# First feed-forward product as 2x2 block products with seven multiplications, and modulation products moved to layer 2

## The chip, the core and the metric

One core of a Trainium2 chip runs the whole program. The metric is device time in microseconds (us) of one execution; the kernel before takes 2892.97 us in the median of three runs, from 2887.84 to 2894.72. The engines are TensorE (PE in the rows; PEld is its weight load), VectorE (DVE), ScalarE (ACT), GpSimd (POOL), and SyncE (SP), which issues all loads and stores. Each engine takes its instructions in the order in which they stand in its queue.

## What is computed

Two layers of a diffusion backbone work on 128 context and 512 latent tokens together, 640 columns. Each layer mixes tokens in three branches (latent attention, gated linear attention, gated DeltaNet) and then applies a SwiGLU feed-forward. Both parts are shifted, scaled and gated by a modulation vector that comes from a condition through its own weights:

```python
mod = silu(cond) @ w_mod[l] + b_mod[l]
sh_a, sc_a, g_a, sh_f, sc_f, g_f = split(mod, 6)
h = h + g_a * mixer(rmsnorm(h, norm_mix) * (1 + sc_a) + sh_a)
xf = rmsnorm(h, norm_ffn) * (1 + sc_f) + sh_f
gu = xf @ ffn_w_in[l]                    # 1024 -> 2 x 2816
h = h + g_f * ((silu(gu[..., :2816]) * gu[..., 2816:]) @ ffn_w_out[l])
```

## The kernel before

Activations stand with 128 channels on the partitions and the 640 tokens along the free axis, in two halves of 320. Every large product is made in three matmuls, to keep float32's precision in a faster format: the weight piece is split by `wsplit` into a rounded part `wh` (ScalarE, L465) and a residue `wl` (GpSimd, L466), the activation likewise into `xh` and `xl`, and `mm_k` (L474) adds wh times xh, wh times xl, wl times xh. A weight piece holds four blocks of 128x128 and so covers 512 of the contracted channels; a tile of a 1024-channel product takes two pieces, 8 blocks x 3 products x 2 halves = 48 matmuls of 320 columns.

The order of these products is fixed: `job` lists them, and class `Stream` (object `G`) emits them piece by piece between other work. Three weight buffers of each kind rotate, so a piece can be split while the two before it are in use; loads run two pieces ahead. `G.to(name)` emits products until the named one is done, `fill` emits as many as a table gives for a place, and when a tile is done its post (a function in `G.posts`) is emitted. A scheduler then sets each engine's order by priorities; steps of the modulation carry a call that keeps them in program order.

The feed-forward has 22 column pairs in two groups of eleven. For pair f, tile `fg` (gate) and tile `fu` (up) are multiplied, `g_post` (L1765, L1766) makes SiLU from a tanh, `u_post` (L1773) multiplies, and `split` (L478 VectorE, L479 GpSimd) makes the operand pair `ah`, `al` of the second product `fo`, which follows each group with eight tiles. `h_update` (L637) adds each into the residual. The feed-forward's input comes from `modulate`, by halves of the tokens, once the norm of the last residual tile is there (`join`); L619 and L622 scale, L624 (ScalarE) and L631 (VectorE) make `xh` and `xl`.

The modulation has 48 columns of 128 for each of two conditions. The first 16 of layer 1 are made by TensorE at the start. All others are dot products on VectorE: one instruction (L549) multiplies a row of weights `wmt` by the condition and sums it, and a short second one reads the sum. Layer 1 makes its 20 next columns between the steps of its DeltaNet chain (rows halved to 512), four more during the output projection `wo`, and in its feed-forward the last eight and all 48 of layer 2 (rows of 1024). Layer 2 makes none itself.

## Time and profile before

| | us |
|---|---|
| median of three runs | 2892.97 |
| span of the profiled execution | 2896.0 |
| chain stage of layer 1, 623.42 to 896.30 | 272.88 |
| chain stage of layer 2, 2058.95 to 2324.19 | 265.24 |
| feed-forward start to the first gate tile's post, layer 2, 2407.60 to 2427.25 | 19.65 |
| pairs 12 to 22 of the first product, layer 1, 1222 to 1377 | 155.00 |
| pairs 12 to 22 of the first product, layer 2, 2650 to 2805 | 155.00 |

For the profiled execution the span is the time that is known, from its first to its last instruction; it lies 3.0 us above the median of the runs. The chain stage runs here from the clearing of a buffer (L1710) to the first operand of the last merge (L1528).

### The profile page before, as it was taken

Reading aid. Unit: us, or ns where it says so; the run is one execution under the profiler, and the core shown is the slowest. Engines: PE = TensorE matmul, PEld = TensorE weight load, DVE = VectorE, ACT = ScalarE, POOL = GpSimd, SP = SyncE. Lnnn points to the kernel's source line nnn. Section 1 sums busy time; section 2 is a strip of 40 time slices with the busy share of each in tenths; the row PEclk is TensorE's granted clock in tenths of the full one; section 3 lists DMA queues with packets and bytes.
Section 4 is the critical chain, followed back from the end, with each engine's and each line's share of the span. In section 5 each row is a group of like instructions: output and inputs, shape, how many; then the busy total and the mean of one; then the engine's idle time right before and its main releaser. Section 6 shows DMA issues by size and latency. Waiting matters only on the chain. (4 is left out here: it accounts for less than half of the span.)

```text
span 2896.0 us, 49763 instructions
## 1 busy us (share of the span) xinstructions
PE 2721.4 (94%) x19444; PEld 2498.5 (86%) x19444; DVE 1542.6 (53%) x2834; ACT 1209.0 (42%) x2276; POOL 1196.0 (41%) x872
## 2 busy tenths in 40 slices
PE   7899999889999999999998899987999999999998
PEld 4788888778779899999988888876877898999998
DVE  4765584747655699177358576556334334211212
ACT  5575655543333522122366645554333344222223
POOL 3543222333325467366445323233333264443443
PEclk9999999999999999999999999998999999999999
DMA  6254433245433355344323534332423231222222
GB/s 207 90 161 141 91 82 94 88 130 168 140 101 127 108 189 177 86 139 156 105 84 110 177 90 97 72 93 73 137 79 88 73 111 59 77 73 78 73 74 83
DMA packets 291834, 317.10 MB, mean 109 GB/s; under 512 B 163696, under 2 KB 174768, under 8 KB 291472
## 3 DMA queue, kind: packets, MB, share of 16 engines
q1 hardware_dynamic: 291600, 313.92, 37.3%
q8 instruction: 154, 2.52, 0.4%
q14 instruction: 80, 0.66, 0.1%
HBM read 266.01 MB, written 47.82 MB: 108 GB/s over the span
## 5 line engine op out<-in xcount | busy, mean ns | idle before, releaser
L466 POOL TENSOR_TENSOR wl<-wr,wh 128x512 fp32r<-128x512 f32 (+1 forms) x576 | 813.9, 1416 | 1307.0 <-ACT wh L465 1177.0
L474 PE MATMUL gm<-xh,wh 128*128 128x320 f32 x3456 | 846.2, 322 | 25.1 <-ACT xh L624 9.4
L474 PE MATMUL gm<-xh,wl 128*128 128x320 f32 x3456 | 826.8, 316 | 13.4 <-POOL wl L466 13.4
L474 PE MATMUL gm<-xl,wh 128*128 128x320 f32 x3456 | 832.5, 317 | 7.2 <-DVE xl L631 4.2
L465 ACT ACTIVATE wh<-wr 128x512 fp32r<-128x512 f32 (+1 forms) x576 | 357.6, 623 | 944.0 <-PE gm L474 648.9
L474 PEld LDWEIGHTS gm<-xh,wh 128*128 128x128 f32 x3456 | 589.6, 192 | 52.5 <-ACT xh L624 14.5
L474 PEld LDWEIGHTS gm<-xl,wh 128*128 128x128 f32 x3456 | 594.3, 192 | 25.0 <-DVE xl L631 9.8
L474 PEld LDWEIGHTS gm<-xh,wl 128*128 128x128 f32 x3456 | 592.6, 192 | 21.7 <-POOL wl L466 15.5
L549 DVE CUSTOM_DVE_ANT_0 ctb<-wmt,cbb 128x1024 f32<-128x1024 f32 (+1 forms) x200 | 298.6, 1493 | 3.4
L637 DVE SCALAR_TENSOR_TENSOR h<-gm,mod,h 128x128 f32<-128x128 f32 x144 | 55.7, 462 | 272.2 <-PE gm L474 266.1
L474 PE MATMUL gm<-ah,wh 128*128 128x320 f32 x704 | 164.6, 310 | 0.5 <-DVE h L637 0.5
L474 PE MATMUL gm<-ah,wl 128*128 128x320 f32 x704 | 164.1, 309 | 0.0
L474 PE MATMUL gm<-al,wh 128*128 128x320 f32 x704 | 163.9, 309 | 0.0
L962 ACT ACTIVATE VN<-ch 64x64 f32<-64x64 f32 x320 | 70.0, 219 | 178.5 <-DVE vs L959 164.5
L474 PEld LDWEIGHTS gm<-ah,wh 128*128 128x128 f32 x704 | 118.7, 188 | 1.6 <-DVE h L637 1.5
L474 PEld LDWEIGHTS gm<-al,wh 128*128 128x128 f32 x704 | 118.5, 188 | 0.2
L474 PEld LDWEIGHTS gm<-ah,wl 128*128 128x128 f32 x704 | 118.5, 188 | 0.0
L1773 DVE TENSOR_TENSOR th<-th,gm 128x640 f32<-128x640 f32 x44 | 36.2, 822 | 149.2 <-PE gm L474 148.4
L1766 DVE SCALAR_TENSOR_TENSOR th<-th,gm 128x640 f32<-128x640 f32 x44 | 35.9, 816 | 138.3 <-ACT th L1765 138.3
L479 POOL TENSOR_TENSOR al<-th,ah 128x640 fp32r<-128x640 f32 x44 | 89.5, 2033 | 28.0 <-DVE ah L478 28.0
L474 PE MATMUL gm<-ol,wh 128*128 128x320 f32 x384 | 99.3, 332 | 1.5 <-POOL ol L479 1.5
L474 PE MATMUL gm<-oh,wh 128*128 128x320 f32 x384 | 98.7, 334 | 0.5 <-DVE gth L1524 0.3
(747 smaller groups left out, 3822.8 us busy)
## 6 DMA issues: line engine op xcount, KB each, us to landing
wr<-in_wall_dram SPq DMA_DIRECT2D x432, 256.0 KB, 3.0
wmt<-in_wmodt_dram SPq DMA_DIRECT2D x60, 512.0 KB, 3.7
wr<-in_wfo_dram SPq DMA_DIRECT2D x64, 256.0 KB, 2.6
wr<-in_wbr_dram SPq DMA_DIRECT2D x48, 256.0 KB, 2.7
wmt<-in_wmodt_dram SPq DMA_DIRECT2D x40, 256.0 KB, 3.2
wm<-in_wmod_dram SPq DMA_DIRECT2D x16, 512.0 KB, 8.3
wr<-in_wfo_dram SPq DMA_DIRECT2D x32, 192.0 KB, 2.4
h<-in_xt_dram SPq DMA_DIRECT2D x16, 320.0 KB, 5.5
```

The costliest lines, as they stand in the source:

```text
L465: se.activation(wh[:, :w], wr[:, :w], AF.Copy)
L466: ge.tensor_tensor(wl[:, :w], wr[:, :w], wh[:, :w], op=ALU.subtract)
L474: pe.matmul(ps[:, c, :HF], w_[:, wsl], x_[kx][:, c * HF:(c + 1) * HF], start=(start and i == 0), stop=(stop and i == 2))
L479: (lo or ge).tensor_tensor(dst_l, src, dst_h, op=ALU.subtract)
L549: ins = ve.tensor_tensor_reduce(self.t, wm, self.c[:, i], 0.5, 0.0, ALU.mult, ALU.add, accum_out=acc[h][:, m - m0, i:i + 1])
L637: ve.scalar_tensor_tensor(hs[d][:, s:e], ps[:, c, s - c * HF:e - c * HF], g[:, d, i:i + 1], hs[d][:, s:e], op0=ALU.mult, op1=ALU.add)
L962: se.activation(VN[d * 64:(d + 1) * 64, h, n], ps[h * 64:(h + 1) * 64, 1], AF.Copy)
L1766: ve.scalar_tensor_tensor(v3(th), v3(th), 1.0, ps, op0=ALU.add, op1=ALU.mult)
L1773: ve.tensor_tensor(v3(th), v3(th), ps, op=ALU.mult)
```

## The change

The first product's weights of one pair, gate above and up below, form a 2x2 block matrix of 128x512 blocks: A11 and A12 for the gate, A21 and A22 for the up part, by the two halves of the contracted channels. The input forms one too: B11 and B21 for the first half of the tokens, B12 and B22 for the second. For 20 of the 22 pairs the four output blocks are now made from seven block products instead of eight, after Winograd: sums of weight blocks S1 to S4 and of input blocks T1 to T4 are multiplied, and the products are combined. A block product is 4 blocks x 3 products x 1 half = 12 matmuls. The first two pairs stay as they were. The 22 pairs now stand in three groups of eight, seven and seven.

The sums S1 to S4 are made per pair on VectorE (L519), the sums T once per layer after the modulation (`token_sums`). Of the seven weight pieces of a pair two have their residue made by GpSimd and five by VectorE (L494). ScalarE copies three partial results out of PSUM (L1933), VectorE combines them (L1939, L1945, L1948) and then makes SiLU and the product (L1951 to L1953). `ah` is now made by ScalarE (L1911) and `al` by VectorE (L1912). Layer 2 now makes its own modulation columns 16 to 47 at the places where layer 1 makes its own, and layer 1's feed-forward makes only its first 16; all rows are halved to 512 there, with three row buffers instead of four.

```diff
-GROUPS = ((0, 11), (11, 22))
+GROUPS = ((0, 8), (8, 15), (15, 22))
+NPL = 2
...
+PRODS = {1: ("A11", "B11", 0, True), 2: ("A12", "B21", 1, True), 6: ("S2", "T2", 0, False), 5: ("S1", "T1", 1, True),
+         7: ("S3", "T3", 0, False), 4: ("A22", "T4", 0, False), 3: ("S4", "B22", 1, False)}
...
+    def product(self, pair, prod, pre=None):
+        wn, xs, bank, start = PRODS[prod]
+        i = self._sub((pair.name, prod), lambda: pair.get(wn), 4, "pool" if prod in (1, 2) else "dve")
+        self.units.append(dict(name=pair.name, i=i, k0=0, kn=4, xs=xs, c=bank, last=prod == 3, pre=pre, prod=prod, start=start))
...
-    def wsplit(wr, kt):
+    def wsplit(wr, kt, lo=None):
...
-            ge.tensor_tensor(wl[:, :w], wr[:, :w], wh[:, :w], op=ALU.subtract)
+            (ve if lo == "dve" else ge).tensor_tensor(wl[:, :w], wr[:, :w], wh[:, :w], op=ALU.subtract)
...
+    class Pair:
+        def __init__(self, name, top, low):
+            self.name, self.t = name, {}
+            self.src = {"A11": top[:, 0:512], "A12": top[:, 512:1024], "A21": low[:, 0:512], "A22": low[:, 512:1024]}
+        def get(self, n):
+            if n not in self.t:
+                if n in self.src:
+                    if n in ("A11", "A12"):
+                        self.t[n] = wload(self.src[n])
+                    else:
+                        with prio("pl"):
+                            self.t[n] = cur["sw"].tile([P, 512], F32, name="wq", tag="wq", bufs=3)
+                            dma(self.t[n], self.src[n])
+                else:
+                    x, y, op = {"S1": ("A21", "A22", ALU.add), "S2": ("S1", "A11", ALU.subtract),
+                                "S3": ("A11", "A21", ALU.subtract), "S4": ("A12", "S2", ALU.subtract)}[n]
+                    x, y = self.get(x), self.get(y)
+                    with prio("pw"):
+                        self.t[n] = cur["sw"].tile([P, 512], F32, name="ws", tag="ws", bufs=5)
+                        ve.tensor_tensor(self.t[n], x, y, op=op)
+            return self.t[n]
+        def fetch(self, *names):
+            for n in names:
+                self.get(n)
+    def mm_block(ps, w, k, xs, start, stop):
+        wsl = slice(k * P, (k + 1) * P)
+        h, l_ = cur["X"][xs]
+        with prio("pg"):
+            for i, (w_, x_) in enumerate(((w[0], h), (w[0], l_), (w[1], h))):
+                pe.matmul(ps, w_[:, wsl], x_[k], start=(start and i == 0), stop=(stop and i == 2),
+                          skip_group_check=True)
...
+    def token_sums(us, sh, xeh, xel, xt1, pool_):
+        h0, h1 = HS
+        for k in range(4):
+            for d in (k, k + 4):
+                for i, s, e in ((0, 0, TP), (1, TP, T)):
+                    se.activation(us[d][:, s:e], us[d][:, s:e], AF.Identity, bias=sh[:, d, i:i + 1])
+            u, v, t1 = us[k], us[k + 4], xt1[:, k]
+            t = pool_.tile([P, 3, HF], F32, name="tsum", tag="tsum", bufs=2)
+            ve.tensor_tensor(t1, u[:, h1], u[:, h0], op=ALU.subtract)
+            ve.tensor_tensor(t[:, 0], v[:, h1], t1, op=ALU.subtract)
+            ve.tensor_tensor(t[:, 1], v[:, h1], u[:, h1], op=ALU.subtract)
+            ve.tensor_tensor(t[:, 2], v[:, h0], t[:, 0], op=ALU.subtract)
+            se.activation(xeh[:, k], t, AF.Copy)
+            ve.tensor_tensor(xel[:, k], t, xeh[:, k], op=ALU.subtract)
...
+            q = pairs[fs[0]]
+            G.product(q, 1, lambda q=q: q.fetch("S1", "S2"))
+            G.product(q, 2, lambda q=q: q.fetch("S3", "S4"))
+            kf = f1 - f0
+            for f in fs:
+                q, n = pairs[f], pairs[f + 1] if f + 1 < f1 else None
+                G.product(q, 6)
+                G.product(q, 5)
+                G.product(q, 7, n and (lambda n=n: n.fetch("A21", "A22")))
+                if n:
+                    G.product(n, 1)
+                else:
+                    fo(0, [(0, 4)])
+                G.product(q, 4, n and (lambda n=n: n.fetch("S1", "S2")))
+                if n:
+                    G.product(n, 2, lambda n=n: n.fetch("S3", "S4"))
+                G.product(q, 3)
+            fo(1, [(0, 4)])
+            fo(0, [(4, kf - 4)])
+            fo(1, [(4, kf - 4)])
+            for d in range(2, 8):
+                n = pairs[f1] if d == 7 and gi + 1 < len(GROUPS) else None
+                fo(d, pre=n and (lambda n=n: n.fetch("A21", "A22")))
...
-                    mst = ModVe(bd, 4, 2).steps(0, range(16, 16 + OPT["mc"])) if l == 0 else iter(())
+                    mst = ModVe(bd, 4, 2).steps(l, range(16, 16 + OPT["mc"]))
...
-        mv = ModVe(mvp, 4, 1) if l + 1 < L else None
+        mv = ModVe(mvp, 3, 2)
...
+        mvs = mv.steps(l, range(16 + OPT["mc"], 40), True)
...
+            own = mv.steps(l, range(40, 48), True)
+            nxt = mv.steps(l + 1, range(16), True) if l + 1 < L else iter(())
...
+            def close(f, f0, f1, th):
+                se.activation(ah[:, f - f0], th, AF.Copy)
+                ve.tensor_tensor(al[:, f - f0], th, ah[:, f - f0], op=ALU.subtract)
+                if f0 == 0:
+                    some(own, 4 if f + 1 < f1 else 1000)
+                    if f + 1 == f1:
+                        mod_fix(mod, prm, 5)
+                elif f1 < NF:
+                    some(nxt, 2)
...
+                def post(prod, ps):
+                    def kept(n):
+                        s_[n] = sn.tile([P, HF], F32, name="sn", tag="sn", bufs=3)
+                        se.activation(s_[n], ps[:, 0, :HF], AF.Copy)
+                    if prod == 1:
+                        kept(1)
+                    elif prod == 2:
+                        g.append(tmp())
+                        ve.tensor_tensor(g[0][:, h0], ps[:, 1, :HF], s_[1], op=ALU.add)
+                    elif prod == 6:
+                        kept(2)
+                    elif prod == 7:
+                        kept(3)
+                        u = sn.tile([P, HF], F32, name="su", tag="su", bufs=1)
+                        ve.tensor_tensor(u, ps[:, 1, :HF], s_[3], op=ALU.add)
+                        g.append(u)
+                    elif prod == 3:
+                        ve.tensor_tensor(g[0][:, h1], ps[:, 1, :HF], s_[2], op=ALU.add)
+                        th = tmp()
+                        se.activation(th, g[0], AF.Tanh, scale=0.5)
+                        ve.scalar_tensor_tensor(th, th, 1.0, g[0], op0=ALU.add, op1=ALU.mult)
+                        ve.tensor_tensor(th[:, h0], th[:, h0], ps[:, 0, :HF], op=ALU.mult)
+                        ve.tensor_tensor(th[:, h1], th[:, h1], g[1], op=ALU.mult)
+                        close(f, f0, f1, th)
+                return post
+            gl_ = len(GROUPS) - 1
...
+            def fo_post(gi, d):
+                def post(ps):
+                    h_update(hs, d, ps, mod[:, 40:48])
+                    some(nxt, 3 if (gi, d) != (gl_ - 1, 7) else 1000)
                 return post
...
+            se.activation(xh[:, 0:4, HF:], xt1, AF.Copy)
+            ve.tensor_tensor(xl[:, 0:4, HF:], xt1, xh[:, 0:4, HF:], op=ALU.subtract)
```

How the change moves instructions, at two places. On ScalarE at the start of layer 1's feed-forward, before: the last pieces of the input (xh, L624) with the weight pieces (wh, L465) between and behind them, then the tanh of the first gate tile.

```order
L624 ACTIVATE xh<-th,mod_102 128x320 x6
L465 ACTIVATE wh<-wr 128x512
L624 ACTIVATE xh<-th,mod_102 128x320 x2
L465 ACTIVATE wh<-wr 128x512
L1765 ACTIVATE th<-gm 128x640
L465 ACTIVATE wh<-wr 128x512 x4
```

The same place now; us are the scaled input tiles, xeh the rounded token sums, wh (L493) the weight pieces of the first two pairs.

```order
L705 ACTIVATE xh<-us_10060,mod_102 128x320
L705 ACTIVATE xh<-us_10061,mod_102 128x320
L715 ACTIVATE us_10058<-us_10058,mod_102 128x512
L715 ACTIVATE us_10059<-us_10059,mod_102 128x128
...
L722 ACTIVATE xeh<-tsum 128x960
L715 ACTIVATE us_10061<-us_10061,mod_102 128x128
L722 ACTIVATE xeh<-tsum 128x960
L715 ACTIVATE us_10061<-us_10061,mod_102 128x512
L493 ACTIVATE wh<-wr 128x512 x2
L1905 ACTIVATE th<-gm 128x640
```

The weight piece that stood ahead of the last two input pieces now stands behind 14 instructions of the token sums, of L715 and L722.

On VectorE in the first group of layer 1, before: a pair's two posts and the cast, then modulation steps of 1024 columns.

```order
L1766 SCALAR_TENSOR_TENSOR th<-th,gm 128x640
L1773 TENSOR_TENSOR th<-th,gm 128x640
L478 CAST ah<-th 128x640
L549 ISA ctb,mod_103<-wmt,cbb 128x1024
L549 ISA mod_103 128x1
L549 ISA ctb,mod_103<-wmt,cbb 128x1024
L549 ISA mod_103 128x1
L549 ISA ctb,mod_103<-wmt,cbb 128x1024
```

Now, in the third pair of the first group: al, wl, su and th are operands of the pairs, L614 the modulation steps of 512 columns; the weight sums (L519) and more residues (L494) stand above and below.

```order
L1951 SCALAR_TENSOR_TENSOR th<-th 128x640
L1952 TENSOR_TENSOR th<-th,gm 128x320
L1953 TENSOR_TENSOR th<-th,su 128x320
L1912 TENSOR_TENSOR al<-th,ah 128x640
L614 ISA ctb,mod_102<-wmt,cbb 128x512
L614 ISA mod_102 128x1
L494 TENSOR_TENSOR wl<-wq,wh 128x512
L614 ISA ctb,mod_102<-wmt,cbb 128x512
L614 ISA mod_102 128x1
L614 ISA ctb,mod_102<-wmt,cbb 128x512
L614 ISA mod_102 128x1
L1945 TENSOR_TENSOR su<-gm,sn 128x320
```

The steps stand after the pair's last residue (L1912), and the residues of the next products (L494) and the partial sum (L1945) now stand between them in the same queue.

## Rows read from the trace of the kernel before

**Rows 1.** The page's first part, the span and the engines' totals
```profile
span 2896.0 us, 49763 instructions
...
PE 2721.4 (94%) x19444; PEld 2498.5 (86%) x19444; DVE 1542.6 (53%) x2834; ACT 1209.0 (42%) x2276; POOL 1196.0 (41%) x872
```

**Rows 2.** Stretches: us, busy us (count) of PE, PEld, DVE, ACT, POOL, clock, DMA
```profile
1222.00:1377.00 155.00, 155.00 (x1059) 155.00 (x1058) 113.87 (x122) 34.37 (x56) 95.12 (x55) 1.00 0.46 144
...
2650.00:2805.00 155.00, 155.00 (x1059) 155.00 (x1058) 31.05 (x35) 34.46 (x56) 72.78 (x54) 1.00 0.26 76
```

**Rows 3.** TensorE's instructions in order: start, us, engine, line, operation; output projection, layer 2
```profile
2394.09 0.31 PE L474 MATMUL gm<-xh,wh 128*128 128x320 f32 x1
...
2397.47 0.31 PE L474 MATMUL gm<-xh,wl 128*128 128x320 f32 x1
```

**Rows 4.** VectorE in order, end of output projection and start of feed-forward, layer 2
```profile
2389.20 0.83 DVE L598 TENSOR_TENSOR nacc<-nacc,th 128x640 f32<-128x640 f32 x1 [0.81 <-ACT th L597]
...
2407.26 0.48 DVE L619 TENSOR_TENSOR th<-us,nacc 128x320 f32<-128x320 f32 x1
...
2427.97 0.82 DVE L1766 SCALAR_TENSOR_TENSOR th<-th,gm 128x640 f32<-128x640 f32 x1 [1.89 <-ACT th L1765]
```

**Rows 5.** VectorE in order, feed-forward of layer 1
```profile
1306.23 0.82 DVE L1773 TENSOR_TENSOR th<-th,gm 128x640 f32<-128x640 f32 x1 [3.09 <-PE gm L474]
...
1308.26 1.21 DVE L549 CUSTOM_DVE_ANT_0 ctb<-wmt,cbb 128x1024 f32<-128x1024 f32 x1
1309.40 0.08 DVE L549 DVE_READ_ACCUMULATOR2_ANT mod<- 128x1 f32 x1
1309.51 2.48 DVE L549 CUSTOM_DVE_ANT_0 ctb<-wmt,cbb 128x1024 f32<-128x1024 f32 x1
...
1312.04 2.20 DVE L549 CUSTOM_DVE_ANT_0 ctb<-wmt,cbb 128x1024 f32<-128x1024 f32 x1
```

**Rows 6.** GpSimd in order, the same stretch
```profile
1306.69 1.30 POOL L466 TENSOR_TENSOR wl<-wr,wh 128x512 fp32r<-128x512 f32 x1 [2.22 <-ACT wh L465]
...
1313.74 1.66 POOL L466 TENSOR_TENSOR wl<-wr,wh 128x512 fp32r<-128x512 f32 x1 [0.58 <-ACT wh L465]
```

**Rows 7.** ScalarE in order, start of the feed-forward, layer 2
```profile
2394.68 0.40 ACT L613 ACTIVATE us<-h,mod 128x128 f32<-128x128 f32 x1
2395.46 0.74 ACT L597 ACTIVATE th<-h 128x640 f32<-128x640 f32 x1 [0.38 <-DVE h L637]
2396.11 0.71 ACT L613 ACTIVATE us<-h,mod 128x512 f32<-128x512 f32 x1
...
2423.28 0.63 ACT L465 ACTIVATE wh<-wr 128x512 fp32r<-128x512 f32 x1 [1.14 <-PE gm L474]
2423.82 1.00 ACT L624 ACTIVATE xh<-th,mod 128x320 fp32r<-128x320 f32 x2
```

**Rows 8.** VectorE in order, the first pair's second half done, layer 2
```profile
2431.70 0.82 DVE L1773 TENSOR_TENSOR th<-th,gm 128x640 f32<-128x640 f32 x1 [2.91 <-PE gm L474]
```

**Rows 9.** Lines by form: shapes xcount | busy us, mean ns | idle before
```profile
L1111 ACT ACTIVATE kbh<-pkn 64x768 fp32r<-64x768 f32 x16 | 12.8, 801 | 5.2 <-DVE kbl L1112 5.0
...
L549 DVE CUSTOM_DVE_ANT_0 ctb<-wmt,cbb 128x512 f32<-128x512 f32 x80 | 69.1, 864 | 0.3
```

**Rows 10.** Stretches, as rows 2: chain stages, output projections and norms, start of feed-forward
```profile
623.42:896.30 272.88, 265.99 (x2219) 218.65 (x2218) 164.96 (x487) 90.85 (x245) 96.74 (x79) 0.99 0.49 136
2058.95:2324.19 265.24, 259.29 (x2210) 214.87 (x2209) 101.14 (x318) 88.38 (x242) 91.32 (x78) 0.99 0.36 97
896.30:998.17 101.87, 95.50 (x592) 90.66 (x590) 64.58 (x98) 51.05 (x91) 56.84 (x38) 0.93 0.43 142
2324.19:2427.25 103.06, 97.27 (x602) 92.23 (x600) 46.47 (x79) 49.83 (x88) 53.39 (x38) 0.93 0.28 89
2407.60:2427.25 19.65, 16.58 (x68) 13.91 (x68) 15.67 (x33) 12.96 (x27) 6.33 (x6) 0.71 0.04 10
```

**Rows 11.** DMA issues: line, engine, operation xcount, KB each, us to landing
```profile
wr<-in_wall_dram SPq DMA_DIRECT2D x432, 256.0 KB, 3.0
```

184 lines of the change are left out of this document (115 added, 69 removed).

## Prediction, made before the changed kernel was run

> **What bounds the kernel now.** I read the page's totals first: TensorE is busy for 94% of the span and no other engine for more than 53% [rows 1]. An average hides stages with other limits, so the view by stretches came next, cut at the edges of the feed-forward in the timeline. The reader should see that the stretch from 1222 to 1377 us, eleven of the 22 column pairs of layer 1's first feed-forward product, has TensorE busy in all of its 155.00 us, and that layer 2's, 2650 to 2805 us, is as long to the digit although VectorE is busy for 113.87 us in one and 31.05 in the other [rows 2]. So TensorE alone sets this stage, and everything else lies beside it. 155.00 us over 1059 matmuls is 0.146 us each; 1056 of them are the eleven pairs, so a pair of 96 costs 14.1 us. The new products use single halves of 320 columns; TensorE already does that at the end of the output projection, where the first and the last of 24 such matmuls start 3.38 us apart, 0.147 each [rows 3]. The price holds for the new form.
>
> **What is removed.** Twenty of the 22 pairs of each layer fall from 96 to 84 matmuls: 12 x 20 x 2 = 480 x 0.1464 = 70.3 us of TensorE time. A pair is then 84 x 0.1464 = 12.3 us of TensorE, if the weights arrive in time. The second product, the first two pairs and the number of their weight pieces do not change.
>
> **What VectorE gets for it.** Per pair the order shows nine instructions of 128x512 (four weight sums at L519, five residues at L494), five of 128x320 (L1939, L1945, L1948, L1952, L1953) and two of 128x640 (L1951, L1912). Prices when GpSimd is out of the way: 0.48 us for 320, 0.83 for 640, hence 0.69 for 512 on the line between [rows 4]. That is 9 x 0.69 + 5 x 0.48 + 2 x 0.82 = 10.3 us. A next instruction that does not wait starts 0.07 before the end of the one before (1308.26 + 1.21 against 1309.40, [rows 5]); over some 14 joins that is 1.0 off, 9.3 us. To this come two waits. The residue at L1912 follows a ScalarE copy of 640 columns that itself follows VectorE's last product, and the queue is in order: the like of it costs 0.81 us of idle time at 2389.20 [rows 4]. And GpSimd: where one of its residues meets VectorE's steps, a step of 1.21 becomes 2.20, 0.99 more, and the residue 1.66 instead of 1.30 [rows 5, 6]. A pair keeps two on GpSimd, and about 0.8 of VectorE's work in it reads SBUF alone (four of the 0.48 read PSUM, and L1773, which does so now, keeps its 0.82 while a residue of GpSimd runs into it and keeps its 1.30 [rows 5, 6]); 2 x 0.99 x 0.8 = 1.6. Together 9.3 + 0.8 + 1.6 = 11.7 us against 12.3 of TensorE: hidden, with 0.6 to spare. The bounds are 10.1 (the two never meet) and 12.6 (both always do, at 2.48 - 1.21 = 1.27 each). ScalarE's seven splits and five other instructions of at most 640 columns are under 7 x 0.63 + 5 x 0.74 = 8.1 us a pair [rows 7] and stay beside it.
>
> **The modulation steps on top of it.** A step of 512 columns is 0.69 plus 0.04 for reading its sum (1309.51 - 1308.26 against 1.21, [rows 5]), 0.73.
> - First group, both layers: the order puts 24 steps and two refreshes of the condition (0.69 each) in the six pairs' rows, 18.9 us or 3.2 a pair. 11.7 + 3.2 = 14.9 against 12.3: VectorE becomes the bound, and as a product's weights are made at most two products ahead (three buffers), nothing averages this out. 2.6 x 6 = 15.6 a layer, 31 us in both. Bounds: 6 a layer from 10.1, 21 from 12.6.
> - Second group, layer 1: 15 steps in seven pairs, 1.6 each; 13.3 against 12.3, 7 us. Bounds 0 and 13.
> - The other groups carry no steps: 0, or up to 0.3 x 21 = 6 us from 12.6. Steps between the second product's tiles hide: such a tile is 48 matmuls, 7.0 us of TensorE, for three steps and one update.
>
> **The start of the feed-forward.** Before, ScalarE makes the weight piece of the first pair's second half at 2423.28, ahead of the last two pieces of the input, and the pair's post comes at 2431.70; TensorE did its last 24 matmuls, 3.5 us, just before, so it began them near 2428.1 [rows 7, 8]. In the new order that piece stands behind the token sums: 14 rows of L715 and L722 lie between the last input piece and it, six of 0.71, five of 0.40 and three of 960 columns (1.0 each, drawn on from 0.80 for 768) [rows 7, 9], 9.3 us. Here too a next one starts 0.09 early (2395.46 + 0.74 against 2396.11), 13 times, and 8.1 us are left; five more lie before the last input piece, in time that ScalarE spends waiting for GpSimd now. The sums that VectorE must finish first (12 of 320 columns and one residue of 960, 6.4 us) keep just ahead of it. Input done near 2425.2, plus 8.1, the piece's own 0.63 and about 0.5 of mutual waits: 2434.4 against 2428.1, 6.3 us without work for TensorE in each layer, 13 us. Bounds: 0 (the sums fit into gaps), and 10 a layer, since after the wait for the norm the clock stands at a mean of 0.71 in these 20 us [rows 10] and a second stop could keep it low.
>
> **The modulation in layer 2.** Its chain stage gets 80 steps of 0.864 us [rows 9]. Layer 1 has had them there all along: from the same clearing of a buffer to the same first merge it takes 272.88 us, layer 2 without them 265.24 [rows 10]. I take the 7.6 difference as their price. Layer 1's output projection, with steps, takes 101.87 against 103.06, so there they hide [rows 10]. Bounds 0 and 15, for the points where this layer's products are filled in were set without them.
>
> **Sum.** -70.3 + 31 + 7 + 13 + 7.6 = -12 us. It is made against the profiled execution (2896.0 us of span); the runs before stand at 2893 in the median, and I move the difference there: **2881 us**.
>
> **Rivals.**
> - VectorE keeps pace. For it: GpSimd does half as much per pair as before, so the two may seldom meet; at 10.1 us a pair, the first group still loses 12 us and the second nothing. -70.3 + 12 + 13 + 7.6 = -38, 2855; with the start hidden as well 2842. Against it: in layer 1 now VectorE's steps of 1024 columns are 1.21, 2.48 and 2.20 one after the other [rows 5], so they do meet when VectorE is full.
> - The meeting costs the whole of GpSimd's instruction each time: pair 12.6, first group 3.5 x 6 x 2 = 42, second 13, the others 6, then -70.3 + 42 + 13 + 6 + 13 + 7.6 = +11, 2904, slower. It decides as soon as a pair without steps exceeds 12.3. For it: one step of 2.48 [rows 5]. Against it: the next costs 0.99. [...]
> - The weights come late. All loads stand in SyncE's one queue; a modulation row waits there until VectorE has used the row three loads before it, and the weight loads behind it wait too. With VectorE 2.6 us late per pair, one landing of 3.0 us [rows 11] would be laid open in each of the first group's six pairs: 2 x 6 x 3.0 = 36, 2881 + 36 = 2917, slower. For it: the order has a modulation row ahead of weight rows throughout that group. Against it: two pieces are always loaded ahead, and with weights landing in 3.0 us TensorE shows no wait for one now.
>
> **Numbers.** Forecast 0.46, VectorE keeping pace 0.24, whole exclusion 0.17, late weights 0.13. The forecast's own range is 2866 to 2896. This kernel's runs spread so that less than 0.3%, about 8.7 us, can't be told from no change; 2884.3 and 2901.7 are the edges. Faster: 0.24 and 0.6 of 0.46, 0.52. Same: 0.35 of 0.46 and 0.2 of 0.17, 0.19. Slower: the rest, 0.29. The range runs from the first rival to the last: 2844 to 2914.
>
> **What the new profile would show.** The matmul count down by 480 and TensorE at 0.146 to 0.147 where it is fed. If I am right: in the first group of both layers a pair near 14.9 us with VectorE busy over 90%, TensorE waiting there for residues of L494; the last group of layer 2 near 12.3 a pair without waits; a stop of 6 us for a weight piece of L493 soon after each feed-forward's start; layer 2's chain stage near 273 us. I am wrong if the first group's pairs run at 12.3 or 13, if pairs without steps lie over 12.6, or if TensorE's waits name a weight's DMA.

## The result and the profile after

The changed kernel takes 2969.45 us in the median (2961.4 to 2970.32) against 2893.84 (2887.84 to 2897.18) for the kernel before, measured beside it: a ratio of 1.025, interval 1.0229 to 1.0271. The forecast was 2881, with a range to 2914. The profiled execution took 2961.4 us, the lowest of the four; its span is 63.3 us longer than before, while the medians lie 75.6 us apart, and the stages below can account for the 63.3 alone.

The totals, as in [rows 1]:

```profile
span 2959.3 us, 50253 instructions
...
PE 2691.0 (91%) x18964; PEld 2439.6 (82%) x18964; DVE 1888.7 (64%) x3712; ACT 1390.0 (47%) x2624; POOL 988.0 (33%) x748
```

The 480 matmuls are gone (19444 to 18964), and TensorE is busy for 30 us less. It is idle for 94 us more, and no other engine comes near its span. So the work became less and the waits more; the stages say where. Their edges are read from TensorE's timeline, where one product's matmuls end and the next one's begin (us; "tiles" are the first product's column tiles of each group, the two products that the order puts between them included; "mixer 2" runs from the end of layer 1's feed-forward to layer 2's output projection; the other names are those of the experiments):

```
                 projection    norm         tiles, layer 1       tiles, layer 2       mixer 2
before           54.1  53.0    9.9   9.9    164.7  154.9         164.7  154.9          895.6
changed          59.1  59.0   17.0  16.5    142.1  104.4   99.8  141.9  100.2  100.1   901.4
1 order held     59.1  59.0   17.1  17.2    144.7  103.8   99.9  144.8  100.3  100.3   905.2
2 table held     58.6  59.3    9.9   9.9    149.0  106.0   99.8  145.1   99.9   99.9   901.9
3 move alone     58.8  58.3   15.5  15.1    164.1  154.9         164.0  154.9          901.6
4 steps early    59.1  53.0   16.0   9.9    141.5  118.0  119.1  132.0   99.8   99.9   893.6
5 sequence       59.0  60.3   15.9  16.3    139.1  101.1   98.2  139.5   98.0   97.6   908.3
6 table in DRAM  53.8  53.7    9.9   9.9    146.0  100.8   99.9  147.2  100.2   99.9   904.4
```

**Pairs without steps.** The last group of layer 2 has no modulation steps and 612 matmuls, 89.9 us at 0.147. Busy time by stretch, columns as in [rows 2]; above the first group of layer 1, below the group without steps:

```profile
991.50:1133.60 142.10, 119.97 (x721) 113.44 (x722) 109.28 (x201) 71.31 (x130) 33.52 (x24) 0.92 0.27 84
...
2796.80:2896.90 100.10, 93.83 (x614) 89.77 (x613) 67.74 (x105) 46.52 (x83) 19.69 (x15) 1.00 0.21 63
```

VectorE, the engine that the forecast watched, is busy for 67.74 us there, 9.7 a pair, and ScalarE for 46.52. Neither fills the stretch, at a clock of 1.00, and yet a pair takes 13.5 to 13.8 us (three restarts lie at 2818.42, 2831.92 and 2845.70) where its 84 matmuls need 12.3. TensorE's waits in this group (us in all, times, longest), and its restart in one pair:

```profile
PE gm L531 <- ACT wh L493: 4.0, 6, 0.9
PE gm L531 <- ACT sn L1933: 1.0, 1, 1.0
PE gm L531 <- DVE th L1939: 0.7, 1, 0.7
PE gm L539 <- ACT wh L493: 0.6, 1, 0.6
```
```profile
2830.99 0.30 PE L531 MATMUL gm<-xeh,wl 128*128 128x320 f32 x1
2831.92 0.42 PE L531 MATMUL gm<-xh,wh 128*128 128x320 f32 x1 [0.62 <-ACT wh L493]
2832.18 0.31 PE L531 MATMUL gm<-xl,wh 128*128 128x320 f32 x1
```

Once a pair TensorE stands: 0.93 us pass between the last matmul of product 6 and the next one, where 0.147 would do, and the matmul after that starts 0.26 later, 0.11 too late. The releaser named is a weight piece. ScalarE at the same time:

```profile
2830.26 0.74 ACT L1950 ACTIVATE th<-th 128x640 f32<-128x640 f32 x1 [0.19 <-DVE th L1948]
2831.24 0.63 ACT L493 ACTIVATE wh<-wr 128x512 fp32r<-128x512 f32 x1 [0.25 <-PE gm L531]
2831.78 0.42 ACT L1933 ACTIVATE sn<-gm 128x320 f32<-128x320 f32 x1
```

The piece belongs to the next pair's product 1: the order has two of its matmuls ahead of product 5. Behind it ScalarE copies product 6's sum out of PSUM to `sn`. Which of the two TensorE needs is what the first experiment asks.

**Output projection and norm.** They take 12.1 us more in layer 1 (59.1 + 17.0 against 54.1 + 9.9) and 12.6 in layer 2. Waits of TensorE there, layer 1, and one of ScalarE:

```profile
PE cs L669 <- DVE nacc L660: 4.8, 1, 4.8
PE gm L539 <- POOL wl L494: 2.4, 4, 0.8
PE cs L669 <- ACT th L664: 2.2, 1, 2.2
PE gm L539 <- ACT wh L493: 1.9, 2, 1.6
```
```profile
ACT ctb L600 <- DMA cbb<-in_condb_dram: 5.5, 2, 3.1
```

And VectorE in order at the end of the projection:

```profile
969.11 1.08 DVE L601 SCALAR_TENSOR_TENSOR cbb<-ctb,cbb 128x512 f32<-128x512 f32 x1 [4.51 <-ACT ctb L600]
...
971.62 1.65 DVE L614 CUSTOM_DVE_ANT_0 ctb<-wmt,cbb 128x512 f32<-128x512 f32 x1
...
975.76 0.69 DVE L614 CUSTOM_DVE_ANT_0 ctb<-wmt,cbb 128x512 f32<-128x512 f32 x1
976.38 0.08 DVE L614 DVE_READ_ACCUMULATOR2_ANT mod<- 128x1 f32 x1
976.38 1.13 DVE L728 SCALAR_TENSOR_TENSOR h<-gm,mod,h 128x128 f32<-128x128 f32 x3
```

Four modulation steps that belong to the feed-forward stand ahead of the residual update (L728) for which the norm waits. `keep_in_program_order` holds a step behind the instruction written just before it, and that is L601, which makes the condition table and is not held itself: it floated up and took the steps along.

**First group.** TensorE's longest waits in layer 1's:

```profile
PE gm L539 <- ACT wh L493: 4.6, 2, 4.0
PE gm L531 <- DVE su L1945: 4.3, 4, 1.9
PE gm L531 <- ACT wh L493: 3.0, 5, 0.6
PE gm L531 <- DVE th L1939: 2.4, 1, 2.4
```

The 4.0 is the piece behind the token sums, where the forecast had 6.3 us for the whole stop; its residue takes 1.9 more. Waits for VectorE's sums `su` and `th` are there too, with VectorE busy for 109.28 of 142.10 us.

Behind the stop TensorE's granted clock is lower too. Stretches of the same group, the first one right behind the stop, and TensorE's rows in it:

```profile
1015.80:1022.60 6.80, 4.93 (x19) 4.86 (x19) 2.64 (x4) 1.80 (x3) 5.35 (x3) 0.50 0.29 83
991.50:1037.00 45.50, 36.83 (x192) 34.38 (x193) 32.88 (x62) 29.77 (x57) 14.93 (x11) 0.77 0.14 43
1037.00:1133.60 96.60, 83.14 (x531) 79.07 (x530) 76.40 (x139) 41.54 (x74) 18.59 (x13) 0.98 0.32 103
```
```profile
1018.45 0.73 PE L539 MATMUL gm<-xh,wh 128*128 128x320 f32 x2
1022.18 0.66 PE L539 MATMUL gm<-xl,wh 128*128 128x320 f32 x2
```

The granted clock is 0.50 there, and matmuls start 0.267 us apart (14 times from 1018.45 to 1022.18), where at 1.00 it is 0.147; all 70 records of the clock in this trace stand at one of these two values. Over the whole group 65 matmuls start at 0.50, 34 in the first group of the kernel before: by the difference of 0.12 us, some 4 us a layer.

### The profile page after: what moved, and what is told of

Its sections match the earlier page's. It is cut to its first block, busy times and chain, and to the rows that moved or that the text cites. A ratio compares the mean times of both kernels' runs of the same rounds, so it can differ in the third digit from the quotient of the medians.

```text
span 2959.3 us, 50253 instructions
## 1 busy us (share of the span) xinstructions
PE 2691.0 (91%) x18964; PEld 2439.6 (82%) x18964; DVE 1888.7 (64%) x3712; ACT 1390.0 (47%) x2624; POOL 988.0 (33%) x748
## 5 line engine op out<-in xcount | busy, mean ns | idle before, releaser
L494 POOL TENSOR_TENSOR wl<-wr,wh 128x512 fp32r<-128x512 f32 x496 | 691.7, 1398 | 1609.1 <-ACT wh L493 1371.5
L539 PE MATMUL gm<-xl,wh 128*128 128x320 f32 x2176 | 543.2, 323 | 11.3 <-DVE xl L707 3.8
L493 ACT ACTIVATE wh<-wr 128x512 fp32r<-128x512 f32 x496 | 305.5, 620 | 490.0 <-PE gm L539 231.5
L539 PEld LDWEIGHTS gm<-xh,wl 128*128 128x128 f32 x2176 | 380.5, 195 | 32.2 <-POOL wl L494 23.7
L539 PEld LDWEIGHTS gm<-xl,wh 128*128 128x128 f32 x2176 | 381.5, 195 | 30.2 <-DVE xl L693 8.1
L614 DVE CUSTOM_DVE_ANT_0 ctb<-wmt,cbb 128x512 f32<-128x512 f32 x320 | 288.2, 901 | 2.8
L531 PE MATMUL gm<-xl,wh 128*128 128x320 f32 x640 | 198.8, 311 | 0.0
L493 ACT ACTIVATE wh<-ws 128x512 fp32r<-128x512 f32 x160 | 101.0, 632 | 175.9 <-PE gm L531 154.5
L531 PE MATMUL gm<-xeh,wh 128*128 128x320 f32 x480 | 152.8, 318 | 17.6 <-DVE su L1945 10.0
L728 DVE SCALAR_TENSOR_TENSOR h<-gm,mod,h 128x128 f32<-128x128 f32 (+2 forms) x192 | 73.2, 432 | 118.8 <-PE gm L539 118.5
L531 PE MATMUL gm<-xel,wh 128*128 128x320 f32 x480 | 148.9, 310 | 0.0
L531 PE MATMUL gm<-xeh,wl 128*128 128x320 f32 x480 | 148.9, 310 | 0.0
```

The costliest lines, as they stand in the source:

```text
L493: se.activation(wh[:, :w], wr[:, :w], AF.Copy)
L494: (ve if lo == "dve" else ge).tensor_tensor(wl[:, :w], wr[:, :w], wh[:, :w], op=ALU.subtract)
L531: pe.matmul(ps, w_[:, wsl], x_[k], start=(start and i == 0), stop=(stop and i == 2), skip_group_check=True)
L539: pe.matmul(ps[:, c, :HF], w_[:, wsl], x_[kx][:, c * HF:(c + 1) * HF], start=(start and i == 0), stop=(stop and i == 2))
L614: ins = ve.tensor_tensor_reduce(self.t, wm, self.c[:, i], 0.5, 0.0, ALU.mult, ALU.add, accum_out=acc[h][:, m - m0, i:i + 1])
L728: ve.scalar_tensor_tensor(hs[d][:, s:e], ps[:, c, s - c * HF:e - c * HF], g[:, d, i:i + 1], hs[d][:, s:e], op0=ALU.mult, op1=ALU.add)
```

## Experiments

Three theories of the loss went in: the order of TensorE's queue (two hoisted matmuls), the supply of weights by ScalarE and VectorE, and the condition table with the steps that it carries.

**1. The order held.** In `mm_block`:

```
-                pe.matmul(ps, w_[:, wsl], x_[k], ...)
+                tc.keep_in_program_order(pe.matmul(ps, w_[:, wsl], x_[k], ...))
```


> All matmuls of the block products are held in the order in which the program writes them; nothing else is changed. Theory of the order: in the changed kernel the first two matmuls of the next pair's product 1 stand ahead of product 5 of the pair at hand, want their weight piece two products early and make TensorE stand for ScalarE. Held in order, a group of seven pairs without modulation steps goes from 100 us to about 90 (612 matmuls of 0.147), a pair from 13.7 to about 12.4, and all 40 pairs give 40 to 55 us: 2915 to 2930 us. Rival, supply: the weight pieces come late in any order, because ScalarE and VectorE take as long for a pair as TensorE; the wait goes to products 5 or 4 instead, a group stays at 98 to 101 us and the time at 2960 to 2970.

2972.6 us, ratio 1.0269 (1.0253 to 1.0286): nothing gained, the order theory falls. But the wait now shows its other face. TensorE's waits in the group without steps; one pair's restart; and product 2's start at the group's head:

```profile
PE gm L531 <- ACT sn L1933: 6.9, 7, 1.2
```
```profile
2841.69 0.30 PE L531 MATMUL gm<-xeh,wl 128*128 128x320 f32 x1
2842.95 0.41 PE L531 MATMUL gm<-xh,wh 128*128 128x320 f32 x1 [0.95 <-ACT sn L1933]
2843.20 0.30 PE L531 MATMUL gm<-xl,wh 128*128 128x320 f32 x1
...
2810.29 0.41 PE L531 MATMUL gm<-xh,wh 128*128 128x320 f32 x1 [0.96 <-ACT sn L1933]
```
```profile
2841.94 0.63 ACT L493 ACTIVATE wh<-wr 128x512 fp32r<-128x512 f32 x1 [0.25 <-PE gm L531]
2842.47 0.42 ACT L1933 ACTIVATE sn<-gm 128x320 f32<-128x320 f32 x1
```

Product 5 starts 0.06 us after ScalarE has copied product 6's sum. It does not use that sum: it writes the other bank of the pair's PSUM tile, from zero. Product 2 likewise waits for the copy of product 1. So the program ties a product to the copy of the one just before it in the same tile, and TensorE pays the round trip, 1.11 us and 0.11 of restart. In the changed kernel the scheduler only filled this hole with two matmuls. It is a wait on a handover, neither on an engine's rate nor on weights. Whether the tie comes from tracking the tile as a whole stays open: a tile for each bank was not tried.

**2. The table held.** Lines 601 and 614 both kept in program order:

```
-                ve.scalar_tensor_tensor(self.c[:, i], self.t, 1.0, ...)
+                ins = ve.scalar_tensor_tensor(self.c[:, i], self.t, 1.0, ...); tc.keep_in_program_order(ins)
```


> The two instructions that make the condition table of a half (line 601) are held in program order, so that the first modulation steps of the feed-forward can no longer stand ahead of the last residual update before the norm. Theory: the gap between the last product of the output projection and the first of the feed-forward goes from 17.0 and 16.5 us back to about 10 in both layers: 13 us less, 2953 to 2959 us. Rival: the six or so instructions only move into the start of the first group, where VectorE is late anyway, and the 13 us come back there: 2966 to 2971 us.

2966.41 us, 1.0248 (1.0229 to 1.0266). The norm gap is 9.9 in both layers, so the floating steps were its cause; but the first groups take 149.0 and 145.1 in place of 142.1 and 141.9. The rival is right about the total. TensorE's waits for `su` grow there (4.3 to 8.0 us in layer 1), and the granted clock falls from 0.92 to 0.89.

**3. The move alone.** The kernel before, with the modulation lines of the changed one, in the main:

```
-        mv = ModVe(mvp, 4, 1) if l + 1 < L else None
+        mv = ModVe(mvp, 3, 2)
+            own = mv.steps(l, range(40, 48), True)
+            nxt = mv.steps(l + 1, range(16), True) if l + 1 < L else iter(())
```


> The kernel before, with its 11 and 11 plain feed-forward products, and with the modulation products placed as in the changed kernel (layer 2's in layer 2: chain, output projection, first group). Theory: the loss around the output projection and the norm belongs to the steps, so this kernel shows it without any block product: about 13 us at the two norms and up to 14 in the two output projections, 2905 to 2921 us against 2893 to 2895 of the kernel before. Rival: the loss there comes with what the block products need (eight prescaled tiles, more GpSimd residues), and the move alone costs under 6 us: 2888 to 2900 us.

2924.69 us, 1.0105 (1.0086 to 1.0125): 32.6 us for the part that the forecast priced at 7.6. Projection and norm cost 10.3 us in layer 1 and 10.5 in layer 2, mixer 2 6.0, and plain first groups nothing (164.1 and 164.0).

**4. Layer 2's steps in layer 1.** Its own lists of steps are empty then:

```
-            nxt = mv.steps(l + 1, range(16), True) if l + 1 < L else iter(())
+            nxt = mv.steps(l + 1, range(48), True) if l + 1 < L else iter(())
-                    some(nxt, 2)
+                    some(nxt, 7 if f + 1 < NF else 1000)   # and in the third group
```


> The changed kernel with all of layer 2's modulation products in layer 1 again, spread over its feed-forward, so that layer 2 has block products and no steps at all. Theory that the steps make the first group and the projection slow: in layer 2 the output projection goes from 86.5 to about 78 us, the gap of the norm from 16.5 to 10, the first group (two plain products and six pairs) from about 138 us to 118, while layer 1's feed-forward, with 128 more steps beside it, grows by 20 to 60 us. Rival: order and supply of the weight pieces alone set the pairs' time; layer 2's first group stays above 130 us and its other two at 100.

2965.69 us, in a single execution. Layer 2 without steps: projection 53.0, norm 9.9, mixer 893.6, first group 132.0 in place of 141.9, the other groups 99.8 and 99.9. So steps cost 10 us in a first group, 6 in the projection and 7 at the norm, and have no part in the pairs' 100; 118 were expected for the first group, and the rival's 130 is nearer. Where layer 1 has seven steps beside each pair, a group takes 118 to 119.

**5. Another sequence of products.** Order held as in 1:

```
-    6, 5, 7, next 1, 4, next 2, 3
+    5, 6, next 1, 7, next 2, 4, 3
```


> Products held in program order as in the first experiment, but in another sequence: 5, 6, next pair's 1, 7, next pair's 2, 4, 3 in place of 6, 5, 7, next 1, 4, next 2, 3. Theory of the shared tile: product 5 waits until ScalarE has read the sum of product 6 out of the same PSUM tile, though out of its other bank; 1.25 us in each pair, which the changed kernel half fills with two matmuls of the next pair. With a product of the next pair between 6 and 7 no product follows directly on what it must wait for: a group without steps goes from 100 us to 90 to 93, all 40 pairs give 40 to 50 us, and the time is 2920 to 2935 us. Rival, supply: ScalarE's and VectorE's work for a pair sets its time in any sequence; product 4 then waits for VectorE's sum instead, a group stays above 96 us and the time above 2950.

2952.59 us, 1.0203 (1.0188 to 1.0218): 20 us less than 1. A pair goes from 13.54 (2829.41 to 2842.95) to 12.82 (2815.07 to 2827.89), so the handover was a cause. By its figures the rival's marks are met, a group over 96 and a time over 2950, but not by its reason: in the last group TensorE's named waits stand at the head (0.9 and 0.7 us) and in the output products (0.6 twice), and none in a pair. The gain is half of what was expected: a single product between is 1.76 us, and copy and sum come 0.11 to 0.17 after it, with 0.11 of restart each; and at the head of each group products 1, 2 and 5 still follow one another directly.

**6. The table from DRAM.** `cdr` is a scratch tile; `cdone` says which half is in it:

```
+            if h in cdone:
+                return dma(self.c, cdr[h])
             dma(self.c, a["condb"][:, :, h * self.w:(h + 1) * self.w])
```


> The changed kernel, with the condition table of a half made once, kept in DRAM and loaded ready made at the ten later places, so that ScalarE's two tanh (line 600) and VectorE's two instructions (line 601) of each half go there; steps and places of the modulation unchanged. Theory: ScalarE stands in its queue behind a tanh that waits for the table's load, and that load for VectorE's steps on the half before, and so the weight pieces are late: output projection from 59 to 54 or 55 us, norm from 17 to 12 or less, together 12 to 22 us: 2947 to 2957 us. Rival: the steps themselves cost it, by VectorE's time and by GpSimd's residues that stretch beside them; projection and norm change by under 3 us, the time stays at 2962 to 2970.

2950.0 us, 1.0191 (1.0174 to 1.0208), as expected. The projection is back at 53.8 and 53.7, the norm at 9.9. TensorE's waits there, layer 1 (lines 6 higher):

```profile
PE cs L675 <- ACT th L670: 1.9, 1, 1.9
PE gm L539 <- ACT xh L711: 1.2, 1, 1.2
PE gm L539 <- POOL wl L494: 0.4, 1, 0.4
```

The steps keep their places in the program; the four that had floated up no longer stand ahead of the residual update, and of the waits for weights 0.4 us is left. Experiment 2 took the four away too and left the projection at 58.6 and 59.3, so the projection's loss is the making of the table: ScalarE's tanh in its queue behind the load (5.5 us, above), with VectorE's two instructions, which this edit takes away together and does not tell apart. 24 us are saved there and 9 given back in the first groups, where the clock falls from 0.92 to 0.89 and 0.90.

**7. Sequence and table together.**

> The two edits of the other kernels of this call together. If their places are apart, as both theories have it, the gains add: 52 to 72 us less than the changed kernel, 2897 to 2917 us. If VectorE's time in the first group is what is short, a part of each comes back there, and the sum is 15 us or more above that of the two alone.

2925.89 us, 1.0108 (1.0092 to 1.0125): 43.6 us less than the changed kernel, where 5 and 6 alone give 16.9 and 19.5. That is less than the 52 to 72 expected, since 5 gave half of what was counted on; but the gains add, with 7 us on top; in the first groups, 139.2 and 138.1, nothing of the table's gain is given back any more.

**8 to 10. Towards a faster one**, on top of 7, each on top of the one before:

```
-NPL = 2
+NPL = 8                                                  # 8
+    'ts': -1000, 'pk': 150,                              # 9: token_sums in prio("ts"), as in 12
-                with self.prio("pp"):
+                with self.prio("pp" if last else "pk"):  # 9: posts of a pair's products
-                    some(own, 4 if f + 1 < f1 else 1000)
+                    some(own, 8 if f < 3 else 1000)      # 10, first group of layer 1
+                    some(nxt, 14 if f > 3 else 0)        # 10, begins with layer 2's 80 chain steps
```

> The kernel with table from DRAM and products in the sequence 5, 6, 1, 7, 2, 4, 3, in which now the whole first group (eight tiles) is taken as plain products, and only the 14 of the second and third group as blocks. Theory: in the first group the blocks lose to VectorE (32 own modulation steps and the token sums' start beside six pairs: 139 us where the matmuls need 105), while plain products leave VectorE free, as in the kernel before, where the first eleven took 164.7 us with a start that costs 10. First group then 8 x 14.1 + 10 + 4 of token sums = 127 us, fo of it 56 us; against 139 + 53 = 192 us this is 183: 9 us less in each layer, 2902 to 2912 us. Rival: the pairs still pay there (six pairs save 10.6 us of matmuls by themselves), so that plain ones give 2925 to 2935.

> As the kernel with a plain first group, with two priorities changed: the reads of a product's sum out of PSUM (line of the copy to sn) may pass other work on ScalarE and VectorE, above all the copy to ah, and the token sums come after everything that is ready. Theory: product 7 no longer waits 0.14 and 4 no longer 0.16 us, with 0.1 each for the restart: 0.25 to 0.5 us a pair, 28 pairs, 7 to 14 us; and the 4 to 5 us by which the first plain products wait for a weight piece behind the token sums on ScalarE go, 8 us in both layers: together 12 to 22 us less than the plain first group alone. Rival: VectorE's sums and not ScalarE's copies are what comes last, and the token sums are needed by then: under 5 us.

> The kernel before this one in this call, with the 80 modulation steps that stand in layer 2's chain stage put into layer 1's plain first group. Theory: layer 2's mixer, 896 us in the kernel before and 902 to 909 in kernels with the steps there, goes back to 896, 6 to 13 us less, and the plain group of layer 1 hides the 80 steps (62 us at 0.77 beside some 25 us of its own work in 127 us). Rival: steps in the first group are paid by weight residues and fo's updates, and it gains nothing.

2918.96 us (ratio 1.0077, 1.0056 to 1.0099), 2897.07 (1.0012, 0.9996 to 1.0028) and 2910.16 (1.0047, 1.0029 to 1.0066). The plain group gives 7 us where 14 to 24 were expected. The priorities give 22: the first groups go from 130.5 and 129.1 to 121.3 and 120.6, which is the stop behind the token sums, 4.8 us for a weight piece in 8 and gone in 9, and what followed on it (1.3 us for the piece's residue, and a clock of 0.93 and 0.94 that is now 0.94 and 0.96); groups without steps stay at 97.4 to 99.0. The last one gains 15 us in mixer 2 (909.6 to 894.9) and pays 23 in layer 1: the first group's output product 66.4 for 56.5, the second group 111.9 for 99.0. That is the rival's account; its profiled execution, 2901.70, lies 8.5 us below its median, so these stages show only a part of the 13 us.

**11. The move alone, table from DRAM.** The kernel of 3 with the edit of 6.

> The kernel before with only the modulation moved (2924.7 us), and with the condition table made once and loaded from DRAM afterwards. Theory: of the 32 us that the move costs without any block product, the two projections and norms hold 21 (58.8 + 15.5 and 58.3 + 15.1 against 54.1 + 9.9 and 53.0 + 9.9), and all of it is ScalarE standing behind the table: 2900 to 2906 us. Rival: the steps as such cost it: 2915 us or more.

2908.76 us, 1.0041 (1.0025 to 1.0056): half of the move's 32 us go, between the 2900 to 2906 expected and the rival's 2915. Projection and norm are as in the kernel before (53.5 and 53.4, 9.9 twice), and so are the feed-forwards; by the profile the rest lies in mixer 2. The profiled execution, at 2921.84, lies 13 us above the median, and its 919.0 for that stage proves nothing; over all kernels with steps there the stage takes 901 to 912, without them 893.6 to 895.6. What sets it within that range stays open.

**12. The sums late in the changed kernel**, with no other edit:

```
-            token_sums(us, mod[:, 24:32], xeh, xel, xt1, up)
+            with prio("ts"):   # 'ts': -1000
+                token_sums(us, mod[:, 24:32], xeh, xel, xt1, up)
```


> The changed kernel with one edit: the token sums are given a later place, so that ScalarE makes the first weight pieces of the feed-forward ahead of the sums' twelve instructions. Theory of the prediction's own term: the first plain products wait 4 to 5 us less in each layer, and no more, since the sums are wanted only after two plain products (28 us): first groups 142 to 137, 8 to 10 us less in all, 2958 to 2962 us. Rival: in this kernel the sums only move into the time in which VectorE is short, beside steps and pairs, and under 4 us come of it; or product 6 of the first pair then waits for them, and it is slower.

2954.26 us, 1.0209 (1.019 to 1.0227): 15 us less than the changed kernel, more than expected. The stages explain little of it: 141.1 and 139.3 for the first groups, 3.6 less. The stop for the piece is gone, and the two plain tiles take 36.6 us in place of 45.5, which is more than the 4 to 5 expected. But the pairs behind them take 104.5 and 102.7 for 96.6. Layer 1, stretches and TensorE's waits for VectorE:

```profile
992.40:1029.00 36.60, 34.07 (x192) 32.04 (x193) 33.57 (x60) 28.15 (x55) 12.93 (x11) 0.82 0.17 51
1029.00:1133.50 104.50, 89.81 (x531) 85.68 (x530) 79.33 (x142) 42.79 (x76) 20.61 (x14) 0.90 0.30 96
```
```profile
PE gm L531 <- DVE su L1946: 4.3, 4, 1.9
PE gm L531 <- DVE th L1940: 3.0, 1, 3.0
```

These waits were there in the changed kernel with 4.3 and 2.4 us, so they are not what took the gain back. The clock is: 0.90 in the pairs in place of 0.98. At 1036.30 it falls to 0.50, near the end of the wait of 3.0 us for `th`, and in all 68 matmuls of the pairs run at 0.50, 13 in the changed kernel; at 0.12 us more for each that is 6.6 of the 7.9 us. So by the stages the size is the rival's, and the reason is neither one's. The two profiled executions differ by 2.4 us and the medians by 15: the changed kernel's is the lowest of its four and this one's the highest, and where the typical executions differ stays open.

**13 and 14. Group starts, and residues without GpSimd**, on top of 9: products 1 and 2 of a group's first pair go between the last three output products of the group before; then, in addition,

```
-        i = self._sub(..., 4, "pool" if prod in (1, 2) else "dve")
+        i = self._sub(..., 4, "dve")
```


> The version with a plain first group, table from DRAM and late sums (2897 us), with products 1 and 2 of a group's first pair put ahead of the last two output products of the group before. Theory: the two waits at a group's start (1.1 and 0.8 us, product 2 for the copy of product 1 out of the same tile, product 5 for VectorE's sum of the two) go, with 0.1 for each restart: 2.1 us for each of four groups, 8 us, 2886 to 2891 us. Rival: weights are not there so early, and it stays at 2894 to 2900.

> The kernel before this one in this call, with the residues of all block products' weights on VectorE, none on GpSimd. [...] Rival: VectorE's added 1.4 us a pair make product 4's or 3's sums late: no gain, or 5 to 10 us slower.

2889.54 us, 0.9982 (0.9971 to 0.9993), and **2881.22 us, 0.9955 (0.9939 to 0.9971)**: the first as expected, the second 8.3 us below it where 5 to 10 were foretold, and faster than both kernels, by 0.45% against the kernel before. Why GpSimd mattered shows in 9, in one of two pairs with a stop of 1.3 us. GpSimd, VectorE and TensorE there (products' lines 12 higher):

```profile
2781.84 1.39 POOL L494 TENSOR_TENSOR wl<-wr,wh 128x512 fp32r<-128x512 f32 x1 [7.25 <-ACT wh L493]
2786.13 1.44 POOL L494 TENSOR_TENSOR wl<-wr,wh 128x512 fp32r<-128x512 f32 x1 [2.89 <-ACT wh L493]
```
```profile
2782.11 1.67 DVE L519 TENSOR_TENSOR ws<-wr,wq 128x512 f32<-128x512 f32 x1
...
2786.74 1.18 DVE L1965 TENSOR_TENSOR th<-th,su 128x320 f32<-128x320 f32 x1
```
```profile
2789.58 0.41 PE L531 MATMUL gm<-xh,wh 128*128 128x320 f32 x1 [1.18 <-ACT sn L1945]
```

VectorE's 0.69 becomes 1.67 and its 0.48 becomes 1.18; ScalarE's copy to `ah` waits for that, and the copy to `sn` behind it in the queue comes late for TensorE. In 14, VectorE takes 1.4 us more work a pair, and the stretch of the last group with its head reads:

```profile
2714.60:2819.10 104.50, 103.34 (x694) 101.30 (x693) 73.30 (x121) 48.34 (x86) 5.84 (x6) 1.00 0.22 71
```

TensorE has 103.34 of 104.50 us, and a pair takes 12.59 (2750.41 to 2763.00). VectorE's forms, 13 first (2725 to 2815 us in both):

```profile
L519 DVE TENSOR_TENSOR ws<-wr,ws 128x512 f32<-128x512 f32 x6 | 6.3, 1053 | 0.0
L1926 DVE TENSOR_TENSOR al<-th,ah 128x640 fp32r<-128x640 f32 x5 | 5.4, 1087 | 0.9 <-ACT ah L1925 0.9
```
```profile
L519 DVE TENSOR_TENSOR ws<-wr,ws 128x512 f32<-128x512 f32 x6 | 4.1, 687 | 0.0
L1926 DVE TENSOR_TENSOR al<-th,ah 128x640 fp32r<-128x640 f32 x6 | 5.0, 826 | 0.3 <-ACT ah L1925 0.3
```

## Why the prediction was wrong

The sign was wrong, and the range missed by 55 us. Term by term, in us of the two profiled spans:

```
                                    foretold   measured   from
480 matmuls                         -70.3      -70.3      counts
pairs without steps                   0        +40        four groups at 100 for 89.9
the same wait in 12 first pairs       0        +14        12 x 1.2 (experiment 1)
first groups else, start included    +44       +39        2 x (142.0 - 105.8 - 9.5) - 14
second group of layer 1, its steps   +7        +4         104.4 - 100.2
chain steps of layer 2               +7.6      +6         901.4 - 895.6
projection and norm                   0        +25        12.1 + 12.6
output products                       0        +4         8 tiles in three groups
sum                                 -12        +62        (63.3 between the spans)
```

(105.8 is 720 matmuls at 0.147, 9.5 what the first group of the kernel before takes over its 1056. That the 12 first pairs pay the same wait is carried over from the other pairs. What the other executions of the changed kernel took longer than this one, some 12 us by the medians, is in no profile. The stated range, to 2914, does not reach its own last rival at 2917.)

- **The failed step: "11.7 us against 12.3 of TensorE: hidden".** VectorE needed 9.7 us a pair, less than I took, and ScalarE 6.6, and TensorE stood all the same. I compared engines' totals, and never followed one value from TensorE to ScalarE and back to the next product in its queue. Two products of one PSUM tile in a row cost a round trip of 1.2 us, 40 times. Experiment 1 names the wait, 5 halves it by sequence alone. The forecast's own sign, pairs without steps over 12.6 us, came true at 13.5 to 13.8. This is also why the rival with VectorE keeping pace fails at 2855: in the pairs without steps its condition came true, its time did not.
- **The second failed step: "so there they hide", of the projection.** I read it from layer 1 of the kernel before, where the condition table is made once. Here it is made anew for each half of each run of steps, with a tanh in ScalarE's queue and a load before it; and its instruction carried steps ahead of the norm. Both stood in the order, and I counted refreshes in the first group alone. Experiment 3 shows it, with 20.8 us of 32 in these stages, and 6 and 11, where they are back within 1 us of the kernel before.
- **First groups: right in place, and in size partly by luck.** The start cost 8.9 us a layer (45.5 against 36.6 in experiment 12) where 6.3 were foretold, the steps 10 (experiment 4) where 15.6 were; the two misses nearly cancel. A part of the start is the clock (0.77 over the two plain tiles, 0.82 in experiment 12), which the forecast had in its bounds and not in its sum. The signs did not come as foretold: VectorE was busy for 77% and not over 90%, and TensorE waited for the sums `su` and `th` more than for residues, so VectorE is late in bursts. Taking one cause away gives less than its price, since later waits grow (2, 6) and the clock is lower behind them (0.89 for 0.92 in 2, 0.89 and 0.90 in 6, 0.90 for 0.98 in the pairs of 12).
- **Second group: right** within 3 us. **Chain steps: right** within 2 us in this execution; over all kernels with steps there the price runs from 6 to 16 us. **Late weights: wrong**; no wait of TensorE in the feed-forward names a load.
- **Whole exclusion by GpSimd: right in kind, wrong in price and place.** The forecast read its rows as less than the whole instruction; in them, and in the changed kernel's trace, the end of GpSimd's instruction sets the end of VectorE's (last section). But a VectorE instruction that comes in the middle waits only for the rest: it took 0.98 and 0.70 us more in the rows of 9, and not 1.27. Pairs without steps did exceed 12.3, the rival's own sign, for another reason: where GpSimd cost time, it acted through ScalarE's queue on the handover, not through VectorE's total (9.7 us a pair and not 12.6), and taking it away gave 8.3 us (14).

## What to carry to other kernels

Fewer matmuls by more additions put values into a chain between engines: before adding up busy times, follow each value that TensorE must get back, and see that a whole product from another PSUM tile stands in each gap. A helper instruction that is not held in order takes along those that are held behind it. Where the saving is 12% of a stage, choose the tiles that get it by what else stands beside them: plain products where the small work is, blocks where it is not (7 us here, experiment 8). And count a stop at more than its length where the clock is lower behind it, as at the two plain tiles here (0.50 for 6.8 us).

## What the runs showed of the hardware

- A stop of TensorE cost more than the wait here: the second matmul after a restart starts 0.25 to 0.26 us after the first in place of 0.147, with the clock at 1.00 (2842.95 to 2843.20 in experiment 1; in the changed kernel so in 80 of the 81 stops ahead of block products with over 0.28 us from start to start).
- VectorE's instructions on SBUF alone and GpSimd's residues held each other up. In the changed kernel's trace 56 such instructions of the pairs (L519, L494, L1951, L1953, L1912) begin while a residue (L494) runs, 0.08 to 1.49 us after it. 55 of them end 0.35 us after the residue (320 columns), 0.55 (512) or 0.68 (640), however early they began, and take up to 1.50, 1.78 and 1.24 us for it: as if held until GpSimd is done, and then some 0.14 us less than they take alone (0.48, 0.69 and 0.82). The last, which began 0.12 us before the residue's end, took its 0.69. Experiment 9 shows the same (2781.84 + 1.39 against 2782.11 + 1.67; 2786.13 + 1.44 against 2786.74 + 1.18). 59 others, with an operand in PSUM (L1945, L1948, L1952), keep 0.48 to 0.49 beside a residue. The other way round, 12 residues begin while one of L519, L494 or L1912 runs, 0.11 to 0.62 us after it: VectorE keeps its 0.68 to 0.69 or 0.82 to 0.83, and the residues take 1.13 to 1.81 us, 1.29 in the median of those without VectorE beside them.
- The rows that the forecast rested on say the same, with two of GpSimd that stand between those of [rows 6]:

```profile
1308.42 2.49 POOL L479 TENSOR_TENSOR al<-th,ah 128x640 fp32r<-128x640 f32 x1 [0.43 <-DVE ah L478]
1310.87 2.28 POOL L466 TENSOR_TENSOR wl<-wr,wh 128x512 fp32r<-128x512 f32 x1
```

The step of 2.48 ends 1.08 us after the first of them, the step of 2.20 ends 1.09 after the second. All 81 steps of 1024 columns that begin while a GpSimd instruction runs, in the kernel before, end 1.08 to 1.17 us after it and take up to 2.48; the four without one beside them take 1.22.
